# A bidirectional SSD scan split in two parts: exponents and chunk states beside the projections, y beside q, k and v

## The chip, the cores and the metric

The kernel runs on one core of a Trainium2 chip. It is one program for TensorE (PE, with its weight loads as PEld), VectorE (DVE), ScalarE (ACT), GpSimd (POOL) and SyncE (SP), which issues most DMAs; ACT issues the rest. Each engine works through its own instructions in order. The metric is the device time of one execution in microseconds.

## The reference

One block of a hybrid encoder on 1024 tokens of 1024 float32 numbers, depth 1. A combined projection makes z, xBC, dt, q, k and v. An SSD group (16 heads of 64, two groups of 8 heads, state 128, chunks of 128 tokens, both directions) and a neighbourhood attention group work on it, and an output projection and an MLP follow. The part that the change touches:

```
h = rmsnorm(x);  z, xbc, dt_raw, q, k, v = split(h @ w_in)
xs, b, c = split(silu(conv5(xbc)));  dt = softplus(dt_raw + dt_bias)
# ssd_chunked, per direction (the backward one on flipped tokens):
a_cum  = cumsum(dt * a, within a chunk)
decay  = exp(where(lower, a_cum[l] - a_cum[s], -inf))
y_diag = ((c @ b.T) * decay) @ (xs * dt)
state  = b.T @ (xs * dt * exp(a_cum[-1] - a_cum))      # one per chunk
h_in   = scan: h = exp(a_cum[-1]) * h + state
y_off  = (c @ h_in) * exp(a_cum)
y = y_f + y_b + d_skip * xs;  g = rmsnorm(y * silu(z)) per group
x = x + concat(g, neighbourhood_attention(q, k, v)) @ w_out
x = x + relu(rmsnorm(x) @ w1)**2 @ w2
```

## The kernel before

There are 8 chunks c and 2 groups g of 8 heads. Matrices are split into a high and a low part (fp32r), and every product is made by three matmuls (mm3, L179).

The first stage normalises and transposes x. Then `xbc` (L429) makes the twelve column tiles of xBC: 48 matmuls each (px), an eviction to ub, a convolution of four operations on DVE and SiLU on ACT. B and C stay in SBUF (bT, cT, bNh, bNl); xs goes through transposes (ptx) to the DRAM tensor xs_dr. `decays` (L330) runs after the first four tiles: it makes dt and its cumulative sums, keeps the factors c1, e1, ed and wd, and stores the sums to cum_dr (L426). Then z is made in 16 tiles of 24 matmuls (pz, L503 to 512), and its SiLU is stored to sz_dr.

The scan and the projections of q, k and v (pq, L686 to 734, 48 tiles of 24 matmuls) share the next stretch. The scan runs over i = 0 to 7 and both groups: `backward(7 - i, g)` and then `forward(i, g)` (L679 to 682). `backward` makes the part inside a chunk for both directions at once. It takes C B^T (pcb, L589). For each half q of the heads it loads a block of the cumulative sums, broadcast to all partitions (rb from cum_dr, L607, 512 KB, two buffers), subtracts c1 on POOL twice (L614), picks the direction by a mask on DVE (copy_predicated, L620), takes the exponential on ACT (L625), multiplies by C B^T on DVE (L627), and multiplies with xs on TensorE (pd, L632). `carried` (L559) gives a direction's y from its state (py), and `decay_state` (L537) brings the state one chunk further: xw = xs * wd on POOL, a split on ACT and DVE (xh, xl), a product (pS), a decay on POOL (L551), an addition on DVE (L552) and a new split (sh, sl). The two directions meet in the middle, so half of the sums go to DRAM (y1_dr) and come back. `gated` (L572) multiplies with SiLU(z), normalises and stores to y_dr.

The order in which each engine gets its instructions isn't the order of the code: the tile framework schedules the whole program by its own model of durations, and the order is then fixed. TensorE gets pq, pS, py and pd in one mixed row. A tile of a pool is used again when its readers are done; a pool that is opened later may lie on the same memory as one that was closed, and its tiles then wait for the old ones.

Before the scan's loop stand 26 DMAs that build the attention's bias table (t1_dr, t2_dr, L524 to 534), on SP.

Of the kernel before, what the change touches and what calls it, by code (L numbers as in the profile page):

```python
# [56 lines left out]
def hymba_block(  # L57
# [66 lines left out]
    y1_dr = dr.tile([NT, P, D], F32, name="y1_dr")  # L124
# [54 lines left out]
    def mm3(pt, ah, al, bh, bl, first, last):  # L179
        nc.tensor.matmul(pt, lhsT=ah, rhs=bh, start=first, stop=False)  # L180
        nc.tensor.matmul(pt, lhsT=ah, rhs=bl, start=False, stop=False)  # L181
        return nc.tensor.matmul(pt, lhsT=al, rhs=bh, start=False, stop=last)  # L182

# [37 lines left out]
    with ExitStack() as ph:  # L221
# [91 lines left out]
        with ExitStack() as p1:  # L313
            qp = p1.enter_context(tc.tile_pool(name="qp", bufs=2, side="right", reuse_waits="tile"))
# [15 lines left out]
            def decays():  # L330
                wraw = qp.tile([P, KD, 32], F32, tag="smxr", name="wraw", bufs=1)
# [32 lines left out]
                bias = qp.tile([P, 2, 16], F32, name="bias", bufs=1)  # L364
                nega = qp.tile([P, 2, 16], F32, name="nega", bufs=1)
# [6 lines left out]
                def tmp(name):  # L372
                    return qp.tile(sm, F32, tag="sm" + name, name=name, bufs=1)
# [49 lines left out]
                cum = qp.tile([P, 256], F32, name="cum", bufs=1)  # L423
# [71 lines left out]
            decays()  # L495
            for ft in range(8):
                xbc((ft,))


            szb = sz_dr.rearrange("c p f -> (c p) f").rearrange(  # L500
                "(i b j) f -> i b j f", b=8, j=8
            )
# [10 lines left out]

        def hb(v):
            return v.unsqueeze(2).broadcast_to([P, 8, HD])

        def h8(v):
            return v.rearrange("p (e d) -> p e d", d=HD)

        with ExitStack() as p2:  # L520
# [14 lines left out]
            st = [[None, None], [None, None]]  # L535

            def decay_state(d, c, g, xw):  # L537
                prev = st[d][g]
                pS = ps_s("pS")
                xh = qp.tile([P, 512], F32R, tag="xh", name="xh", bufs=1)  # L540
                xl = qp.tile([P, 512], F32R, tag="xl", name="xl", bufs=1)
                nc.scalar.activation(xh, xw, AF.Copy)
                nc.vector.tensor_tensor(xl, xw, xh.bitcast(F32), op=sub)
                mm3(pS, bNh[:, c, g, :], bNl[:, c, g, :], xh, xl, True, True)
                new = prev and prev[0]
                if prev is None:
                    new = qp.tile([P, 512], F32, tag=f"st{d}{g}", name="st", bufs=1)
                    nc.vector.tensor_copy(new, pS)
                else:
                    dec = ed[:, d, c, 8 * g : 8 * g + 8]  # L550
                    nc.gpsimd.tensor_tensor(h8(new), h8(new), hb(dec), op=mul)  # L551
                    nc.vector.tensor_tensor(new, new, pS, op=add)  # L552
                sh = qp.tile([P, 512], F32R, tag=f"sh{g}", name="sh", bufs=1)
                sl = qp.tile([P, 512], F32R, tag=f"sl{g}", name="sl", bufs=1)
                nc.scalar.activation(sh, new, AF.Copy)
                nc.vector.tensor_tensor(sl, new, sh.bitcast(F32), op=sub)
                st[d][g] = (new, sh, sl)

            def carried(d, c, g):  # L559
                py = ps_s("py")  # L560
                ct = cT[:, g, c * P : (c + 1) * P]
                ch = qp.tile([P, P], F32R, tag="ch", name="ch", bufs=2)
                cl = qp.tile([P, P], F32R, tag="cl", name="cl", bufs=2)
                nc.scalar.activation(ch, ct, AF.Copy)
                nc.vector.tensor_tensor(cl, ct, ch.bitcast(F32), op=sub)
                mm3(py, ch, cl, *st[d][g][1:], True, True)
                yo = qp.tile([P, 512], F32, tag="yo", name="yo", bufs=1)
                e = e1[:, d, c, 8 * g : 8 * g + 8]
                nc.vector.tensor_tensor(h8(yo), h8(py), hb(e), op=mul)
                return yo  # L570

# [11 lines left out]
            def backward(c, g):  # L583
                hs = slice(8 * g, 8 * g + 8)
                cs = slice(c * P, (c + 1) * P)
                xs = qp.tile([P, 512], F32, tag="xs", name="xs")
                nc.sync.dma_start(xs, xs_dr[c, :, g * 512 : (g + 1) * 512])
                pcb = ps_s("pcb")
                nc.tensor.matmul(  # L589
                    pcb[:, 0:P], lhsT=bT[:, g, cs], rhs=cT[:, g, cs], start=True, stop=True  # L590
                )
                cb = pcb[:, 0:P]
# [8 lines left out]
                )  # L601
                pd = ps_v("pd")
                for q in range(2):
                    h0 = 8 * g + 4 * q
                    rb = qp.tile([P, 2, 4, P], F32, tag="rb", name="rb", bufs=2)
                    r0 = c * 16 + h0
                    nc.sync.dma_start(  # L607
                        rb.rearrange("p d h s -> p d (h s)"),
                        cum_dr[:, r0 : r0 + 4, :]
                        .rearrange("d h s -> d (h s)")  # L610
                        .partition_broadcast(P),
                    )
                    for d in range(2):
                        nc.gpsimd.tensor_tensor(  # L614
                            rb[:, d],
                            rb[:, d],
                            c1[:, d, c, h0 : h0 + 4].unsqueeze(2).broadcast_to([P, 4, P]),
                            op=sub,
                        )
                    nc.vector.copy_predicated(  # L620
                        rb[:, 0],
                        lmask.unsqueeze(1).broadcast_to([P, 4, P]),
                        rb[:, 1],
                    )
                    nc.scalar.activation(rb[:, 0], rb[:, 0], AF.Exp)  # L625
                    gm = rb[:, 0]
                    nc.vector.tensor_tensor(  # L627
                        gm, rb[:, 0], cb.unsqueeze(1).broadcast_to([P, 4, P]), op=mul
                    )
                    for j in range(4):  # L630
                        e = 4 * q + j
                        nc.tensor.matmul(  # L632
                            pd[:, e * HD : (e + 1) * HD],
                            lhsT=gm[:, j, :],
                            rhs=xs[:, e * HD : (e + 1) * HD],
                            start=True,
                            stop=True,
                        )
                y1 = qp.tile([P, 512], F32, tag="y1", name="y1")
                nc.gpsimd.tensor_tensor(h8(y1), h8(xs), hb(cf), op=mul)  # L640
                if c < NT - 1:
                    yo = carried(1, c, g)
                    nc.gpsimd.tensor_tensor(y1, y1, yo, op=add)
                nc.vector.tensor_tensor(y1, y1, pd, op=add)
                if c >= NT // 2:
# [89 lines left out]

# [680 lines left out]
```

## Time and profile before

| | |
|---|---|
| median of 3 runs | 1672.34 us (1671.72 to 1681.54) |
| the profiled execution | 1682.42 us, of it 1680.6 us in the span |
| mean granted TensorE clock | 0.984 |
| busy in the span | PE 1596.8, PEld 1301.1, DVE 1031.1, ACT 722.1, POOL 727.7 us |
| first and last product of z | 178.6, 267.2 us |
| first and last product of q, k, v | 267.7, 675.9 us |
| DMA | 274.01 MB, 163 GB/s over the span |

A busy time of TensorE holds the latency of its pipeline, so a row of matmuls shows as fully busy even where each comes 0.23 us after the one before and lasts 0.39. In the rows of groups, "out<-in xcount" names what is written and read, then the busy time of the group in us and the mean of one in ns, then the idle time of the engine just before, and what ended it. In the rows of stretches the engines' busy times stand in order, and behind them the granted clock, the busy share of the 16 DMA engines and GB/s. "DMA issues" gives the KB of one transfer and the median time from issue to landing.

### The profile page before, as it was taken

What the parts mean: (1) busy time and instruction counts of PE and PEld (TensorE: products, weight loads), DVE (VectorE), ACT (ScalarE), POOL (GpSimd) and SP (SyncE); (2) the same over time, 40 slices, a digit from 0 to 9 for tenths busy, and PEclk for the clock granted to TensorE, in tenths of its full rate; (3) what the DMA queues carried; (4) which work ended last, traced back from release to release, by engine and by line L of the source; (5) the groups of instructions that cost most, each with busy time, mean ns of one, the idle gap of its engine ahead of it and who ended that gap; (6) DMA issues with size and microseconds to landing.
All of it is one profiled execution on the core that took longest, in us unless ns stands there. A gap on an engine that the chain in (4) does not pass through costs nothing. (4 is left out here: it accounts for less than half of the span.)

```text
span 1680.6 us, 20886 instructions
## 1 busy us (share of the span) xinstructions
PE 1596.8 (95%) x7461; PEld 1301.1 (77%) x7461; DVE 1031.1 (61%) x1438; ACT 722.1 (43%) x1195; POOL 727.7 (43%) x522
## 2 busy tenths in 40 slices
PE   6999999999988889999999989999999979999999
PEld 5788888777776678887887867788888868888887
DVE  5776314788886853566675567444343387887863
ACT  5434223334343432566566533544444544433330
POOL 4000003877787861233335233344444464455551
PEclk9999999999999999999999999999999999999999
DMA  8213336866675885978565241353344386644231
GB/s 207 61 38 104 90 99 195 218 195 186 226 231 176 221 256 192 275 201 221 167 183 169 89 150 51 113 178 136 138 163 151 114 294 243 213 151 150 100 101 75
DMA packets 180290, 274.01 MB, mean 163 GB/s; under 512 B 14603, under 2 KB 105819, under 8 KB 180187
## 3 DMA queue, kind: packets, MB, share of 16 engines
q1 hardware_dynamic: 136203, 231.77, 45.1%
q10 hardware_dynamic: 42976, 37.23, 7.3%
q0 software_dynamic: 1008, 3.67, 0.5%
q8 instruction: 59, 0.97, 0.2%
q14 instruction: 44, 0.36, 0.1%
HBM read 189.40 MB, written 86.56 MB: 164 GB/s over the span
## 5 line engine op out<-in xcount | busy, mean ns | idle before, releaser
L762 POOL TENSOR_TENSOR wl<-wraw,wh 128x1024 fp32r<-128x1024 f32 x110 | 299.7, 2736 | 317.6 <-ACT wh L761 303.1
L761 ACT ACTIVATE wh<-wraw 128x1024 fp32r<-128x1024 f32 x110 | 115.6, 1054 | 151.2 <-PE px L747 51.2
L747 PE MATMUL px<-wh,ahl 128*128 128x512 f32 x512 | 160.8, 391 | 4.6 <-ACT ahl L761 3.3
L180 PE MATMUL pq<-wh,hTh 128*128 128x512 f32 x384 | 154.3, 404 | 5.7 <-ACT wh L150 5.6
L181 PE MATMUL pq<-wl,hTh 128*128 128x512 f32 x384 | 153.8, 402 | 3.8 <-DVE wl L151 3.8
L747 PE MATMUL px<-h,wh 128*128 128x512 f32 x496 | 156.0, 396 | 1.4 <-DVE x L1103 1.4
L182 PE MATMUL pq<-wh,hTl 128*128 128x512 f32 x384 | 153.4, 401 | 0.0
L762 DVE TENSOR_TENSOR ahl<-ar,ahl 128x1024 fp32r<-128x1024 f32 x56 | 115.1, 2062 | 22.9 <-ACT ahl L761 21.8
L761 ACT ACTIVATE ahl<-ar 128x1024 fp32r<-128x1024 f32 x56 | 58.2, 1052 | 140.0 <-PE px L747 74.7
L747 PEld LDWEIGHTS px<-wh,ahl 128*128 128x128 f32 x512 | 96.0, 188 | 25.9 <-ACT ahl L761 3.7
L747 PEld LDWEIGHTS px<-h,wh 128*128 128x128 f32 x496 | 93.2, 188 | 24.0 <-ACT h L186 1.6
L151 DVE TENSOR_TENSOR wl<-wraw,wh 128x1024 fp32r<-128x1024 f32 x40 | 54.0, 1355 | 82.3 <-ACT wh L150 81.7
L747 PE MATMUL px<-wl,ahl 128*128 128x512 f32 x256 | 99.8, 390 | 0.0
L747 PE MATMUL px<-h,wl 128*128 128x512 f32 x248 | 98.1, 396 | 0.0
L180 PEld LDWEIGHTS pq<-wh,hTh 128*128 128x128 f32 x384 | 74.1, 193 | 22.2 <-ACT wh L150 7.2
L181 PEld LDWEIGHTS pq<-wl,hTh 128*128 128x128 f32 x384 | 74.0, 193 | 20.9 <-DVE wl L151 6.2
L614 POOL TENSOR_TENSOR rb<-rb,c 128x512 f32<-128x512 f32 x64 | 76.6, 1218 | 21.8 <-DMA rb<-cum_dr 21.7
L182 PEld LDWEIGHTS pq<-wh,hTl 128*128 128x128 f32 x384 | 73.9, 192 | 15.2
L186 ACT ACTIVATE pth<-ptp 128x384 fp32r<-128x384 f32 (+1 forms) x128 | 56.8, 456 | 67.3 <-PE ptp L961 66.7
L747 PE MATMUL pz<-h,wh 128*128 128x512 f32 x256 | 82.0, 401 | 0.7 <-DVE h L187 0.7
L150 ACT ACTIVATE wh<-wraw 128x1024 fp32r<-128x1024 f32 x58 | 61.1, 1056 | 46.3 <-PE px L181 19.2
L747 PE MATMUL pz<-wh,ahl 128*128 128x512 f32 x256 | 80.5, 390 | 0.0
(271 smaller groups left out, 4087.5 us busy)
## 6 DMA issues: line engine op xcount, KB each, us to landing
ar<-act_dr SPq DMA_DIRECT2D x56, 512.0 KB, 3.7
act_dr<-cq SPq DMA_DIRECT2D x49, 512.0 KB, 3.2
wraw<-in_w_in_dram SPq DMA_DIRECT2D x44, 512.0 KB, 4.5
rb<-cum_dr SPq DMA_DIRECT2D x32, 512.0 KB, 7.1
wraw<-in_w_mlp_in_dram SPq DMA_DIRECT2D x32, 512.0 KB, 4.6
wraw<-in_w_mlp_out_dram SPq DMA_DIRECT2D x32, 512.0 KB, 5.5
q_dr<-hl ACTq DMA_DIRECT2D x64, 128.0 KB, 3.2
k_dr<-hl ACTq DMA_DIRECT2D x16, 512.0 KB, 5.3
```

The costliest lines, as they stand in the source:

```text
L150: nc.scalar.activation(hi[:, 0:n], raw[:, 0:n], AF.Copy)
L151: lo_eng.tensor_tensor(lo[:, 0:n], raw[:, 0:n], hi[:, 0:n].bitcast(F32), op=sub)
L180: nc.tensor.matmul(pt, lhsT=ah, rhs=bh, start=first, stop=False)
L181: nc.tensor.matmul(pt, lhsT=ah, rhs=bl, start=False, stop=False)
L182: return nc.tensor.matmul(pt, lhsT=al, rhs=bh, start=False, stop=last)
L186: nc.scalar.activation(hi, src, AF.Copy)
L614: nc.gpsimd.tensor_tensor(rb[:, d], rb[:, d], c1[:, d, c, h0 : h0 + 4].unsqueeze(2).broadcast_to([P, 4, P]), op=sub,)
L747: nc.tensor.matmul(pt, lhsT=a, rhs=b, start=f, stop=l, skip_group_check=True)
L761: nc.scalar.activation(hl[0], src, AF.Copy)
L762: eng.tensor_tensor(hl[1], src, hl[0].bitcast(F32), op=sub)
```

## The change

The scan is split. The exponents that `backward` made, up to the mask but without the exponential, are made by `segment` and stored to a DRAM tensor seg_dr: four blocks after each of the eight x tiles in the code. The chunk states of both directions are made by `state`, one chunk of each direction after each of the first 14 tiles of z, and every state that a chunk starts from is stored to st_dr. Each pS is told to stand behind the z tile's last product (`issue_after`).

The rest is one step per chunk and group, first all of g = 0, then all of g = 1. `prepare` loads xs, the two exponent blocks and the states, takes the exponential on ACT and splits C and the states. `inside` makes C B^T, both directions' py, the product of exponents and C B^T, and sums y in SBUF. `finish` makes pd behind a tile of q, k or v, and gates. `prepare` of the next step is called ahead of `finish`, and two or three tiles of q, k and v are made per step. y1_dr, with its 14 stores and 14 loads, is gone. The small tiles of `decays` now lie inside two tiles (`room`) that have the exponents' tag rb, so that both use the same two buffers.

By count the program keeps its matmuls. C is split 16 times in place of 28. SP has 120 DMAs more: 32 stores and 32 loads of exponents, 28 and 28 of states, 14 more loads of xs, and 14 loads of y1 less; ACT issues 14 stores less.

```diff
+            def segment(g, c, q):
+                h0 = 8 * g + 4 * q
+                rb = rp.tile([P, 2, 4, P], F32, tag="rb", name="rb")
+                r0 = c * 16 + h0
+                nc.sync.dma_start(
+                    rb.rearrange("p d h s -> p d (h s)"),
+                    cum_dr[:, r0 : r0 + 4, :]
+                    .rearrange("d h s -> d (h s)")
+                    .partition_broadcast(P),
+                )
+                for d in range(2):
+                    nc.gpsimd.tensor_tensor(
+                        rb[:, d],
+                        rb[:, d],
+                        c1[:, d, c, h0 : h0 + 4].unsqueeze(2).broadcast_to([P, 4, P]),
+                        op=sub,
+                    )
+                nc.vector.copy_predicated(
+                    rb[:, 0],
+                    lmask.unsqueeze(1).broadcast_to([P, 4, P]),
+                    rb[:, 1],
+                )
+                nc.sync.dma_start(
+                    seg_dr[g, c, :, q], rb[:, 0].rearrange("p h s -> p (h s)")
+                )
+
+            segs = [(g, c, q) for g in range(2) for c in range(NT) for q in range(2)]
             for ft in range(8):
                 xbc((ft,))
+                for sg in segs[4 * ft : 4 * ft + 4]:
+                    segment(*sg)
...
+            def state(d, c, g, xs, mark):
+                hs = slice(8 * g, 8 * g + 8)
+                xw = qp.tile([P, 512], F32, tag="xw", name="xw")
+                nc.gpsimd.tensor_tensor(h8(xw), h8(xs), hb(wd[:, d, c, hs]), op=mul)
+                xh = qp.tile([P, 512], F32R, tag="xh", name="xh")
+                xl = qp.tile([P, 512], F32R, tag="xl", name="xl")
+                nc.scalar.activation(xh, xw, AF.Copy)
+                nc.vector.tensor_tensor(xl, xw, xh.bitcast(F32), op=sub)
+                pS = ps_s("pS")
+                with tc.issue_after(mark):
+                    mm3(pS, bNh[:, c, g, :], bNl[:, c, g, :], xh, xl, True, True)
+                prev = st.get((d, g))
+                new = qp.tile([P, 512], F32, tag=f"st{d}", name="st")
...
+                st[d, g] = new
+                nc.sync.dma_start(st_dr[d, g, c + 1 - 2 * d], new)
...
                     for k in range(KD):
                         s = (slice(None), k, slice(t * P, (t + 1) * P))
-                        mm3(pt, hTh[s], hTl[s], *get(k), k == 0, k == KD - 1)
+                        mark = mm3(pt, hTh[s], hTl[s], *get(k), k == 0, k == KD - 1)
...
+                    if 8 * g + t < 14:
+                        states(8 * g + t, mark.ins)
...
+                for q in range(2):
+                    gm = qp.tile([P, 4, P], F32, tag=f"gm{q}", name="gm")
+                    nc.sync.dma_start(gm.rearrange("p h s -> p (h s)"), seg_dr[g, c, :, q])
+                    nc.scalar.activation(gm, gm, AF.Exp)
+                    gms.append(gm)
...
+            for n, (c, g) in enumerate(steps):
+                xs, gms, chl, sts = held
+                y1 = inside(c, g, *held)
+                if n + 1 < len(steps):
+                    held = prepare(*steps[n + 1])
+                mark = next(units)
+                finish(c, g, xs, gms, y1, mark)
+                for _ in range(1 + n % 2):
+                    mark = next(units)
```

The order on SP, from the store of the cumulative sums on. xs_dr takes the x tiles, wraw are weights of z. Before:

```order
L426 DMA cum_dr_75<-cum_711 128x128 x2
L149 DMA wraw_1383<-in_w_in_dram 128x2x512
L488 DMA xs_dr_70<-xn_783 128x8x128
L488 DMA xs_dr_70<-xn_865 128x8x128
L149 DMA wraw_1389<-in_w_in_dram 128x2x512
L488 DMA xs_dr_70<-xn_947 128x8x128
```

And now, where each rb tile is a block of exponents (two buffers, taken in turn):

```order
L446 DMA cum_dr_76<-room_611 128x128 x2
L521 DMA rb_794<-cum_dr_76 128x2x512
L521 DMA rb_800<-cum_dr_76 128x2x512
L150 DMA wraw_1576<-in_w_in_dram 128x2x512
L508 DMA xs_dr_70<-xn_780 128x8x128
L539 DMA seg_dr_71<-rb_794 128x512
L521 DMA rb_806<-cum_dr_76 128x2x512
L539 DMA seg_dr_71<-rb_800 128x512
L508 DMA xs_dr_70<-xn_886 128x8x128
L521 DMA rb_812<-cum_dr_76 128x2x512
```

A block's load stands behind the store of the block that had its buffer, and the x tiles' stores stand between them.

On TensorE, at the same place in z, behind its 115th product. Before, z goes on alone, from one weight tile (wh, wl) to the next:

```order
L181 MATMUL pz_1507<-wl_1385,hTh_90 128x512
L182 MATMUL pz_1507<-wh_1384,hTl_91 128x512
L180 MATMUL pz_1507<-wh_1390,hTh_90 128x512
L181 MATMUL pz_1507<-wl_1391,hTh_90 128x512
L182 MATMUL pz_1507<-wh_1390,hTl_91 128x512
```

Now the first two chunk states stand there, one for each direction:

```order
L181 MATMUL pz_1826<-wh_1583,hTh_91 128x512
L181 MATMUL pS_1624<-xh_1620,bNh_98 128x512
L182 MATMUL pz_1826<-wl_1584,hTh_91 128x512
L181 MATMUL pS_1639<-xh_1635,bNh_98 128x512
L182 MATMUL pS_1624<-xl_1621,bNh_98 128x512
L183 MATMUL pS_1624<-xh_1620,bNl_99 128x512
```

Of the 84 products of pS, 69 stand in z and 15 among the first 63 products of q.

On POOL, behind the x tiles' small fills. Before, nothing stood there until the scan:

```order
L435 MEMSET ub_1295 128x2
L436 MEMSET ub_1295 128x2
L523 MEMSET zt_1871 128x192
L640 TENSOR_TENSOR y1_1930<-xs_1899,cf_1905 128x512
L655 TENSOR_TENSOR xw_1934<-xs_1899,wd_103 128x512
```

Now, within z, exponent blocks (rb), weighted inputs (xw) and decayed states (st) take turns:

```order
L528 TENSOR_TENSOR rb_1230<-rb_1230,c1_101 128x512 x2
L567 TENSOR_TENSOR st_1762<-st_1702,ed_103 128x512
L554 TENSOR_TENSOR xw_1812<-xs_1810,wd_104 128x512
L567 TENSOR_TENSOR st_1806<-st_1746,ed_103 128x512
L554 TENSOR_TENSOR xw_1856<-xs_1854,wd_104 128x512
L528 TENSOR_TENSOR rb_1236<-rb_1236,c1_101 128x512 x2
```

Fifteen blocks stand on POOL and DVE ahead of the first xw and xl, and twelve more before the xw of the last state that z's part of TensorE's order needs.

More of the change, by code (lines that the diff above doesn't have):

```diff
@@ L330, in decays, with slot @@
             def decays():
-                wraw = qp.tile([P, KD, 32], F32, tag="smxr", name="wraw", bufs=1)
+                room = [rp.tile([P, 4, 256], F32, tag="rb", name="room") for _ in range(2)]
+                slots = ["xr", "na", "u", "tt", "t2", "pl", "la", "cum"]
+                def slot(name):
+                    i = slots.index(name)
+                    return room[i // 4][:, i % 4]
+                wraw = slot("la").rearrange("p (k f) -> p k f", f=32)
                 nc.sync.dma_start(
@@ L500, in hymba_block, with states @@
+            def states(n, mark):
+                g, i = n // 7, n % 7
+                for d, c in ((0, i), (1, NT - 1 - i)):
+                    xs = qp.tile([P, 512], F32, tag="xs", name="xs")
+                    nc.sync.dma_start(xs, xs_dr[c, :, g * 512 : (g + 1) * 512])
+                    state(d, c, g, xs, mark)
+            pa.close()
+            qp = p1.enter_context(tc.tile_pool(name="zv", bufs=2, side="right", reuse_waits="tile"))
             szb = sz_dr.rearrange("c p f -> (c p) f").rearrange(
@@ L534, in hymba_block @@
                 )
[L535 to L570, printed above, removed]
             def gated(y1, c, g):
@@ L601, in backward @@
                 )
-                pd = ps_v("pd")
[L603 to L631, printed above, removed]
@@ new lines, in inside @@
+                y1 = qp.tile([P, 512], F32, tag="y1", name="y1")
+                nc.gpsimd.tensor_tensor(h8(y1), h8(xs), hb(cf), op=mul)
+                for gm in gms:
+                    nc.vector.tensor_tensor(
+                        gm, gm, cb.unsqueeze(1).broadcast_to([P, 4, P]), op=mul
+                    )
+                for d in sts:
+                    yo = qp.tile([P, 512], F32, tag="yo", name="yo")
+                    nc.vector.tensor_tensor(h8(yo), h8(pys[d]), hb(e1[:, d, c, hs]), op=mul)
+                    nc.gpsimd.tensor_tensor(y1, y1, yo, op=add)
@@ L632, in backward, with finish @@
+                return y1
+            def finish(c, g, xs, gms, y1, mark):
+                pd = ps_v("pd")
+                with tc.issue_after(mark):
+                    for e in range(8):
                         nc.tensor.matmul(
                             pd[:, e * HD : (e + 1) * HD],
-                            lhsT=gm[:, j, :],
+                            lhsT=gms[e // 4][:, e % 4, :],
                             rhs=xs[:, e * HD : (e + 1) * HD],
@@ new lines, in hymba_block @@
+            units = qkv_units()
+            steps = [(c, g) for g in range(2) for c in range(NT)]
+            held = prepare(*steps[0])
+            mark = next(units)
[7 more added lines that the diff above has]
+                for _ in range(1 + n % 2):
+                    mark = next(units)
@@ L743, in hymba_block @@
+            for mark in units:
+                pass
     ORD = (1, 2, 6, 5, 7, 3, 4)
```

161 lines of the change are left out of this document (80 added, 81 removed).

## The prediction

> **What bounds the kernel now.** I read the slices of the page first, then the stretches around the scan, then who waits for whom on TensorE.
>
> ```profile
> span 1680.6 us, 20886 instructions
> PE   6999999999988889999999989999999979999999
> ```
>
> ```profile
> core 0: us, PE busy (x) PEld busy (x) DVE busy (x) ACT busy (x) POOL busy (x), PEclk, DMA share, GB/s
> 130.00:267.50 137.50, 137.50 (x640) 114.46 (x639) 49.62 (x44) 45.19 (x55) 0.70 (x9) 1.00 0.34 95
> 267.50:676.00 408.50, 372.68 (x1748) 300.10 (x1747) 289.68 (x419) 155.48 (x271) 285.63 (x266) 0.97 0.73 215
> ```
>
> TensorE is the bound nearly everywhere. The weak place is 267.5 to 676, in which the scan runs beside q, k and v: 35.8 us idle (408.5 - 372.7), and a granted clock of 0.97, which costs 12 us of 408.5. Just before it, in 130 to 267.5 (last x projections and z), TensorE never stops, DVE is busy for 36% and POOL for 0.7 us. The change carries work from the second stretch into the first.
>
> How long must the second stretch be? Rows of the timeline give the rate, and three groups the small products:
>
> ```profile
> 270.16 0.39 PE L181 MATMUL pq<-wl,hTh 128*128 128x512 f32 x1
> ...
> 272.65 0.39 PE L180 MATMUL pq<-wh,hTh 128*128 128x512 f32 x1
> ```
>
> ```profile
> L632 PE MATMUL pd<-xs,rb 128*128 128x64 f32 x256 | 33.2, 278 | 7.7 <-DVE rb L627 6.8 <-issue 0.6
> L476 PE MATMUL ptx<-ident,acc 128*128 128x128 f32 x64 | 8.4, 272 | 0.0
> ```
>
> From 270.16 to 272.65 are 11 intervals: a 128x512 product takes 0.226 us of TensorE, whatever its 0.39 us of latency. The stretch has 1152 of pq, 84 of pS and 84 of py: 1320 x 0.2264 = 299 us. With 33 for pd and 17 for the 128 transposes of q and k (32 groups of four, at 8.4/16 each) it needs about 350 of its 408. So 58 us are loss, and this is all that the change can win there. The waits say whose loss:
>
> ```profile
> PE pcb L589 <- DVE yo L569: 7.7, 4, 2.9
> PE pd L632 <- DVE rb L627: 6.8, 6, 2.3
> PE pq L180 <- ACT wh L150: 5.6, 3, 2.9
> PE pq L181 <- DVE wl L151: 3.8, 6, 1.2
> PE pcb L589 <- DVE st L552: 3.0, 1, 3.0
> PE py L180 <- DVE st L552: 1.6, 2, 1.4
> PE ptq L707 <- DVE qn L701: 1.5, 3, 0.9
> PE pS L180 <- ACT rb L625: 1.4, 2, 0.8
> PE py L181 <- DVE sl L556: 0.9, 2, 0.6
> PE pS L180 <- DVE st L552: 0.9, 1, 0.9
> ```
>
> The scan's own waits (pcb, pd, py, pS) are 7.7 + 6.8 + 3.0 + 1.6 + 1.4 + 0.9 + 0.9 = 22.3 of the 35.8 us. The weights' (wh, wl) are 9.4; these stay.
>
> **Part by part: the scan behind its preparation.** The carried recurrence leaves this stretch, and 69 of the 84 pS products (15.6 us of TensorE) go to z, which is neutral. Of the 58 us I let the scan's share go, 22.3/35.8 = 62%: 36 us. Bounds: 22 (only the named waits), and 48 (all but the weights' 9.4). What can come late instead is pd: its exponents are now loaded, go through ScalarE's exponential and DVE's product with cb, and ScalarE and DVE have q, k and v's evictions queued behind a late load. The first step also follows the last stored exponents, and sixteen bias copies on the same queue stand ahead of its second half:
>
> ```profile
> 276.08 12.52 SPq L531 DMA_DIRECT2D t_dr<-t_dr  x16
> ```
>
> I take 3 us for it all, from nothing (loads are asked for one step ahead, some 21 us) up to 2 us in each of 16 steps, 32. The net gain of the stretch is 33 us, between -10 and 48.
>
> **The exponents beside the projections.** Now what hangs on segment. One exponent block is a load of 512 KB, two subtractions on POOL, one copy_predicated on DVE, and a store of 256 KB, and with two rb buffers its buffer is loaded again only when that store has landed. Before, no store stood in this loop. The rows:
>
> ```profile
> 128.70 0.81 SPq L426 DMA_DIRECT2D cum_dr<-cum  x2
> 399.67 1.26 SPq L607 DMA_DIRECT2D rb<-cum_dr  x2
> 420.11 0.41 SPq L607 DMA_DIRECT2D rb<-cum_dr  x1
> ```
>
> ```profile
> 405.54 2.04 POOL L614 TENSOR_TENSOR rb<-rb,c 128x512 f32<-128x512 f32 x2 [3.61 <-DMA rb<-cum_dr]
> 426.18 2.04 POOL L614 TENSOR_TENSOR rb<-rb,c 128x512 f32<-128x512 f32 x2 [0.92 <-DMA rb<-cum_dr]
> ```
>
> ```profile
> L614 POOL TENSOR_TENSOR rb<-rb,c 128x512 f32<-128x512 f32 x64 | 76.6, 1218 | 21.8 <-DMA rb<-cum_dr 21.7
> L620 DVE COPY_PREDICATED rb<-lmask,rb 128x512 f32<-128x512 int32 x32 | 41.7, 1304 | 16.2 <-POOL rb L614 16.2
> L620 DVE COPY_PREDICATED rb<-lmask,rb x32: 714/1554/1827, 280.4 to 598.6; 128x512 f32<-128x512 int32 x32
> L551 POOL TENSOR_TENSOR st<-st,ed 128x512 f32<-128x512 f32 x24 | 28.3, 1180 | 0.6 <-DVE sl L556 0.6
> L655 POOL TENSOR_TENSOR xw<-xs,wd 128x512 f32<-128x512 f32 x14 | 15.1, 1079 | 2.8 <-DMA xs<-xs_dr 2.8
> L542 ACT ACTIVATE xh<-xw 128x512 fp32r<-128x512 f32 x28 | 17.5, 625 | 39.5 <-PE pS L182 12.0 <-POOL xw L655 8.1 <-PE pq L182 5.2
> ```
>
> ```profile
> rb<-cum_dr SPq DMA_DIRECT2D x32, 512.0 KB, 7.1
> wraw<-in_w_in_dram SPq DMA_DIRECT2D x44, 512.0 KB, 4.5
> sz_dr<-zs ACTq DMA_DIRECT2D x16, 256.0 KB, 2.8
> y_dr<-y ACTq DMA_DIRECT2D x24, 256.0 KB, 5.4
> ```
>
> POOL, idle and waiting for the load, began 5.9 and 6.1 us after the issue: 6.0. Two subtractions take 2.0, the copy 1.3, a store of this size 2.8 (sz_dr, written in the quiet z stage), two issues 0.8. The loop is 12.9 us, so 6.5 us per block. Bounds: 4.5 + 2.0 + 0.7 + 2.8 + 0.8 = 10.8, and 7.1 + 2.4 + 1.3 + 5.4 + 0.8 = 17.0.
>
> The order puts fifteen blocks on POOL and DVE ahead of the first chunk state, and TensorE's first pS behind 115 of z's products. cum_dr is issued by 129.5 and should land about 132 (2.8 us, as sz_dr). The fifteenth block is the eighth turn of its buffer: 132 + 7 x 12.9 + 6.0 + 2.0 + 1.3 = 231.6. Then xw (1.1) and xh (0.6): pS can start at 233. z begins at 178.6:
>
> ```profile
> L180 PE MATMUL pz<-wh,hTh x128: 389/389/481, 178.6 to 267.0; 128*128 128x512 f32 x128
> ```
>
> Without waits TensorE is at its first pS at 178.6 + 115 x 0.2264 + 2.1 (16 transposes) = 207. It stalls 26 us (bounds: 10 with the short loop, 57 with the long). The same lateness reaches it by DVE too, whose convolutions and evictions are queued behind the copies; I count it once.
>
> From there to the end of z: TensorE has 269 pz + 69 pS = 338 x 0.2264 = 76.5 us. POOL has 24 subtractions, 23 xw and 18 decays: 24 x 1.22 + 23 x 1.08 + 18 x 1.18 = 75 us. The block loop has 12 turns of 6.5, 77 us. All three are level, so nothing hides anything. The transfers are worse: 12 x 0.79 MB of blocks, 23 xs and some 22 states of 0.26, 11 sz of 0.26 and about 2 MB of weights make 26 MB. The scan's stretch moved 215 GB/s at a share of 0.73, which is 294 at one: 88 us. I add 12 us here, from 0 up to 12 x 8.5 - 76.5 = 25.
>
> ```profile
> 620.00:640.00 20.00, 16.31 (x70) 12.85 (x69) 9.10 (x11) 6.25 (x9) 7.67 (x7) 0.91 1.10 336
> ```
>
> (This row is the most that the trace moved, 336 GB/s; at that rate the 26 MB take 77 us.) So z ends 38 us later than its work asks, between 10 and 82.
>
> The Trainium skill, "DMA: Bandwidth & Descriptors", section "Anatomy of one DMA — SWDGE (gpsimd) path", puts a transfer at about 2.0 us plus its bytes at 436 GB/s; an estimate from that page is 3.2 us for the load and 2.6 for the store, a loop of 9.9 and a stall of 3 us in place of 26, and the sum would then be 3 + 12 - 33, a gain of 18 us. The trace disagrees for this load: 5.9 and 6.1 us.
>
> Other edits: 14 saves and 14 loads of y1 go, 12 splits of C go, 120 DMAs come on SP; the sizes stand in the terms above. The NA stage and the MLP keep their order and cost.
>
> **The sum.** +26 + 12 - 33 = +5 us against the profiled execution: 1682.4 + 5 = 1687. Its span is 1680.6 with 1.8 around it, and the median of the runs shown, 1672.3, lies 10 below it; on that scale the forecast is 1677. A measurement of this kernel can tell about 1% (17 us) from no change.
>
> **Rivals.** *The blocks are short enough* (the side of a gain): with the loop of 10.8 the stall is 10 us, and at 336 GB/s the rest of z costs 1; with the 36 us of the scan's own waits gone and no new one, 10 + 1 - 36 = -25: 1647. For: the new loads come one at a time rather than in pairs, and the share around 130 to 267.5 was 0.34; the page named above says the same. Against: both quoted loads stand in the stretch with a share of 0.73, and this change brings the x and z stage to the same or above. It decides below a loop of about 11.5 us. *The block loop is long*: stores land like y_dr (5.4) and loads like the group's 7.1, 17.0 in all: 57 + 25 - 33 = +49, 1721. It becomes slower by more than 1% from a loop of about 14 us, 1.1 more than I take. For: 26 MB in 77 to 88 us is the fullest DMA of the program. *The scan finds a new wait*: pd waits 2 us in each step, or the first y step starts late: 38 - 36 + 32 = +34, 1706. For: ScalarE now waits in its queue for a load in each step; against: 21 us of notice. That the work is not moved is excluded by the order.
>
> **Chances and range.** Forecast 0.38 (its own range 1656 to 1689, within 1%), short blocks 0.30, long blocks 0.21, new wait in the scan 0.11. Hence faster 0.30, same 0.38, slower 0.32. The range cuts the ends of both sides: 1640 to 1712.
>
> **What would show it.** In the profile after: POOL idle in the x and z stage for "DMA rb<-cum_dr", spaced 6.5 us; the first pS near 233 and the last z product near 320 where work alone gives 283; a stretch of q, k, v and y of about 355 us with the waits of pcb, pd and py for st, sl and rb gone, and those for wh and wl left. A first pS near 215 means short blocks, one past 250 long ones. I am wrong in kind if z stays unbroken, or if the scan's stretch still loses over 50 us.

## The result, and the profile after

The changed kernel takes 1703.74 us (median of 4 runs, 1699.28 to 1705.71) against 1672.77 us before (4 runs on the same chip): a ratio of 1.0163, with an interval of 1.0140 to 1.0186. It is slower by 1.6%, inside the range, but not the case that I held the likeliest. The profiled execution took 1705.05 us, 1703.3 of them in the span, 22.6 more than the profiled one before.

The first two parts of the page after, the span and TensorE's slices:

```profile
span 1703.3 us, 21105 instructions
PE   6999778998999998999999989899999979999999
```

The shallow hole of the kernel before (the 8s of slices 12 to 15, in the scan) is gone; a deeper one stands in slices 5 to 7, ahead of and in z. Four stretches show where the time went. The columns are those of the prediction's rows; first the kernel before, then the changed one:

```profile
130.00:200.00 70.00, 70.00 (x341) 58.55 (x340) 42.27 (x38) 29.57 (x36) 0.70 (x9) 1.00 0.39 110
200.00:240.00 40.00, 40.00 (x179) 33.15 (x178) 4.90 (x4) 9.06 (x11) 0.00 (x0) 1.00 0.35 99
240.00:430.00 190.00, 178.24 (x844) 144.19 (x843) 130.43 (x193) 66.79 (x110) 123.78 (x111) 0.97 0.69 194
430.00:700.00 270.00, 245.29 (x1149) 197.48 (x1147) 175.75 (x264) 108.08 (x200) 170.65 (x162) 0.97 0.73 218
```

```profile
130.00:200.00 70.00, 61.92 (x289) 50.42 (x288) 47.52 (x44) 25.60 (x30) 25.69 (x28) 0.98 0.68 188
200.00:240.00 40.00, 23.67 (x92) 18.59 (x91) 11.58 (x12) 5.92 (x9) 12.64 (x12) 0.77 0.71 181
240.00:430.00 190.00, 166.65 (x701) 129.19 (x701) 125.72 (x154) 61.22 (x97) 135.23 (x116) 0.93 0.89 275
430.00:700.00 270.00, 264.30 (x1323) 222.38 (x1322) 149.31 (x244) 106.06 (x179) 113.59 (x119) 0.99 0.69 209
```

From 430 us on TensorE hardly stops any more: 264 of 270 us busy, against 245. Before 430 it loses far more. The tiles of the changed kernel say where (min, median and longest ns, first and last start):

```profile
L181 PE MATMUL pz<-wh,hTh x128: 388/390/777, 188.7 to 332.6; 128*128 128x512 f32 x128
...
L181 PE MATMUL pS<-xh,bNh x28: 386/394/795, 236.4 to 359.3; 128*128 128x512 f32 x28
...
L183 PE MATMUL pq<-wh,hTl x384: 387/390/629, 337.3 to 697.3; 128*128 128x512 f32 x192
```

z begins 10 us later than before (178.6), the first pS comes at 236.4, and z ends at 333. TensorE's waits, first from 120 to 320 us (x and z), then from 320 to 720 (the scan):

```profile
PE pS L181 <- ACT xh L557: 14.1, 4, 10.1
PE ptx L496 <- ACT acc L488: 12.3, 3, 6.0
```

```profile
PE pq L181 <- DVE hl L195: 5.7, 1, 5.7
PE py L181 <- DMA q_dr<-hl: 4.6, 1, 4.6
PE pq L182 <- DVE wl L152: 3.7, 4, 2.0
PE pS L181 <- ACT xh L557: 2.0, 2, 1.6
PE pd L689 <- DVE gm L676: 1.4, 1, 1.4
```

ptx waits for the convolution, pS for the chain xw, xh behind the exponent blocks. The convolution is late because VectorE stands idle in front of masked copies whose block POOL has not finished (21.6 us from 130 to 210), with the convolution's operations (acc) next in its queue. VectorE's rows, and TensorE's behind them:

```profile
DVE rb L534 <- POOL rb L528: 21.6, 7, 6.3
```

```profile
199.41 0.76 DVE L534 COPY_PREDICATED rb<-lmask,rb 128x512 f32<-128x512 int32 x1 [3.78 <-POOL rb L528]
200.05 2.61 DVE L484 SCALAR_TENSOR_TENSOR acc<-ub,pcol,acc 128x1024 f32<-128x1024 f32 x2
206.46 0.73 DVE L534 COPY_PREDICATED rb<-lmask,rb 128x512 f32<-128x512 int32 x1 [3.80 <-POOL rb L528]
207.07 2.59 DVE L484 SCALAR_TENSOR_TENSOR acc<-ub,pcol,acc 128x1024 f32<-128x1024 f32 x2
```

```profile
210.81 1.97 PE L496 MATMUL ptx<-ident,acc 128*128 128x128 f32 x8 [5.99 <-ACT acc L488]
```

The scan's chains of pcb, pd and py are gone but for single waits.

**One measure for all runs.** Every kernel here gives TensorE the same products. I give each instruction of the trace the usual distance to the next of its kind (0.226 us for a 128x512 product; 1523 us in all, the same for all kernels), add these up for what has started by a time t, and take the sum from t. What is left I call the fall-behind. It counts waits and slow clock alike, in the profiled execution:

```
us behind at t =        130   200   240   430   700   first pS  copies after 240
before                   24    24    24    48    90     280.8
after                    25    36    56    98   109     236.4      17
```

The last column counts the exponent blocks whose masked copy comes after 240 us. So of the 85 us that the changed kernel loses from 130 to 700 us, 11 lie by 200 us, 20 from there to 240 (waits of 6.0 us for ptx and 10.3 for the first pS, and slow products behind both), 42 between there and 430, and 12 in the rest; before it was 0, 0, 24 and 42. That is 19 us more; the other 4 of the 23 come outside this stretch. These are single executions: that of the kernel before lies 9.7 us above its median, so a difference to its row is uncertain by as much, that of half_load_four below lies 7 us under its median and that of one_subtraction 6 above.

### The profile page after: what moved, and what is told of

The parts are those of the page before. It is cut to its first block, busy times and chain, and to the rows that moved or that the text cites. A ratio compares the mean times of both kernels' runs of the same rounds, so it can differ in the third digit from the quotient of the medians.

```text
span 1703.3 us, 21105 instructions
## 1 busy us (share of the span) xinstructions
PE 1599.2 (94%) x7461; PEld 1304.5 (77%) x7461; DVE 1027.5 (60%) x1426; ACT 718.5 (42%) x1183; POOL 724.1 (43%) x522
## 5 line engine op out<-in xcount | busy, mean ns | idle before, releaser
L534 DVE COPY_PREDICATED rb<-lmask,rb 128x512 f32<-128x512 int32 x32 | 38.9, 1216 | 81.3 <-POOL rb L528 78.1
L906 POOL TENSOR_TENSOR mb<-braw,nam 128x256 f32<-128x256 f32 (+1 forms) x48 | 38.5, 832 | 114.4 <-DVE nmx L963 57.1
L151 ACT ACTIVATE wh<-wraw 128x1024 fp32r<-128x1024 f32 x58 | 60.6, 1054 | 55.6 <-DMA wraw<-in_w_in_dram 21.6
```

Source lines behind the costliest of these rows:

```text
L151: nc.scalar.activation(hi[:, 0:n], raw[:, 0:n], AF.Copy)
L534: nc.vector.copy_predicated(rb[:, 0], lmask.unsqueeze(1).broadcast_to([P, 4, P]), rb[:, 1],)
L906: nc.gpsimd.tensor_tensor(mb[:, s].rearrange("p (s r c) -> p s r c", r=16, c=8), v[:, a:b], nam[:, s].rearrange("p (s r c) -> p s r c", r= ...
```

## The experiments

Each run stands beside runs of the kernel before on its chip; the ratio is to these, with its interval. All start from the changed kernel; the last three of the list make the exponents in the scan.

```
                        us      ratio (interval)          130   200   240   430   700   first pS  copies after 240
the change            1703.7   1.0163 (1.0140-1.0186)      25    36    56    98   109     236.4      17
three_buffers         1682.0   1.0027 (1.0012-1.0043)      26    41    57    78    93     241.9      13
four_buffers          1684.3   1.0042 (1.0025-1.0058)      23    41    57    77    91     235.8       8
one_subtraction       1686.8   1.0063 (1.0041-1.0084)      24    40    59    83    98     234.3      14
late_blocks_two       1706.3   1.0182 (1.0146-1.0217)      24    36    40    95   114     215.8      19
late_blocks_four      1682.3   1.0035 (1.0021-1.0048)      23    41    48    77    91     225.9      14
late_blocks_four_8    1683.5   1.0043 (1.0028-1.0058)      24    35    39    78    91     214.6      20
half_load_four        1672.7   0.9968 (0.9951-0.9985)      23    41    58    64    77     237.9       3
no_store_four         1676.5   0.9992 (0.9976-1.0008)      22    44    58    70    84     247.5       2
half_load_late        1676.3   0.9995 (0.9979-1.0011)      24    30    34    72    87     209.5      19
transfers_only        1696.1   1.0124 (1.0103-1.0144)      23    23    43    65   100     223.3
states_only           1668.1   0.9947 (0.9930-0.9965)      22    22    23    44    76     202.0
states_two_ahead      1665.8   0.9933 (0.9911-0.9955)      22    23    23    44    70     202.1
```

**More buffers, less work on POOL, and the exponents back in the scan.** four_buffers and three_buffers give the exponents' tag more buffers:

```diff
-                rb = rp.tile([P, 2, 4, P], F32, tag="rb", name="rb")
+                rb = rp.tile([P, 2, 4, P], F32, tag="rb", name="rb", bufs=4)
```

> Exponent blocks turn on four buffers in place of two; nothing else is edited. Theory LOOP (each buffer's round of load, POOL, VectorE, store and next load, 13.4 us measured in the changed kernel, holds the z stage): four buffers give 13.4/4 = 3.4 us a block; the order now has 23 blocks ahead of the first state's xw on POOL, so the first pS comes about 131 + 23 x 3.4 + 5 = 214 us (236 in the changed kernel) and the other nine blocks fit beside z, whose last product comes near 290 (333); time about 1665 us (1655 to 1680). Rival POOL (its own 75 us of subtractions and 28 xw in the z stage hold it) and rival BYTES (about 26 MB between 200 and 335 us at some 300 GB/s hold it): the work and the bytes are the same, so the first pS may be earlier but z's last product stays past 320, and the time stays at 1690 to 1705.

> Exponent blocks turn on three buffers. LOOP: 13.4/3 = 4.5 us a block, 20 blocks ahead of the first xw in the order, first pS near 131 + 20 x 4.5 + 5 = 226 us, the other 12 blocks take 54 us beside 77 us of z; last product of z near 305, time about 1678 us, between two buffers and four. POOL and BYTES: 1690 to 1705, as with four.

one_subtraction makes half of POOL's subtractions:

```diff
-                for d in range(2):
+                for d in range(1):
                     nc.gpsimd.tensor_tensor(
```

> Each exponent block makes one subtraction on POOL in place of two (the backward direction's is left out, so the exponents above the diagonal are not the reference's); buffers, loads and stores as in the changed kernel. LOOP: a buffer's round is 1 us shorter (12.4), 6.2 us a block; the order has 17 blocks ahead of the first xw, where the changed kernel has 15, so the first pS comes near 131 + 17 x 6.2 + 5 = 241 us, no sooner than now (236); time 1695 to 1708 us. POOL: 32 x 1.2 = 38 us of its work gone, about 20 of it in the z stage: last product of z near 312, time 1675 to 1685. BYTES: unchanged, 1700 to 1706.

states_only takes `segment` and seg_dr out; `prepare` loads and makes the exponents itself:

```diff
-                    gm = qp.tile([P, 4, P], F32, tag=f"gm{q}", name="gm")
-                    nc.sync.dma_start(gm.rearrange("p h s -> p (h s)"), seg_dr[g, c, :, q])
+                    rb = qp.tile([P, 2, 4, P], F32, tag=f"gm{q}", name="rb")
...
+                    gm = rb[:, 0]
+                    nc.vector.copy_predicated(
...
                     nc.scalar.activation(gm, gm, AF.Exp)
```

> The chunk states stay beside z and the scan keeps its one pass, but the exponents are made in the scan again, one step ahead, from the cumulative sums, with their two subtractions, the masked copy and the exponential; nothing is stored of them. LOOP: z is unbroken but for a few us (first pS near 210 us, last product of z 275 to 285). If the scan's gain of 30 us comes from the new order of the pass (ORDER), the scan stretch stays at 360 to 368 us and the time is 1645 to 1658. If it comes from the exponents' having left the scan (EXPONENTS), the scan stretch goes back to 390 to 408 us and the time is 1672 to 1690.

Two buffers more take 1.2 points off, so the round of a buffer was part of the cost; but four buffers end 4 us above LOOP's range and 6 below that of POOL and BYTES, and LOOP named the wrong place. It had counted the planner's new order (23 and 20 blocks ahead of the first xw in place of 15) and still expected the first pS at 214 and 226. It stays at 236 and 242, for a block took some 4.4 us with four buffers and 5.4 with three, not 3.4 and 4.5. one_subtraction speaks against LOOP, which expected no gain: 1.0 point, or 17 us, of the 19 to 29 us that POOL promised. From 240 to 430 us that kernel falls behind by 25 us in place of 42. It makes 14 blocks there, so 14 subtractions of some 1.0 us less on POOL.

states_only shows the price of the exponents' new place: with them in the scan the kernel is 0.5% faster than before. Its z is unbroken:

```profile
L180 PE MATMUL pS<-xh,bNh x28: 390/393/393, 202.0 to 290.8; 128*128 128x512 f32 x28
...
L180 PE MATMUL pq<-wh,hTh x384: 387/389/792, 284.7 to 661.2; 128*128 128x512 f32 x192
```

The scan stretch, 376.5 us, lies between the two theories' bounds: 32 us less than before (where 78 pS, 18 us, have moved to z), and still 15 more than with the change. Of TensorE's loss from 240 to 700 us, 65 before, the states' leaving and the new order of the pass take 12 (to 53), if the 9.7 us by which that execution was long lie elsewhere. The exponents' leaving takes up to 34 more (half_load_four below, with nearly all blocks made by 240, loses 19 there), but they have to be made somewhere.

**Another order.** If the blocks ahead of the first xw set its time, fewer of them there should help. These three tie later blocks on POOL behind the xw of a z tile:

```diff
-                for sg in segs[4 * ft : 4 * ft + 4]:
+                for sg in segs[16 * ft // 8 : 16 * (ft + 1) // 8]:
                     segment(*sg)
...
+                    with tc.issue_after(held[0]):
+                        for sg in late[n * 1 // 1 : (n + 1) * 1 // 1]:
+                            segment(*sg)
```

> Four exponent buffers, and the order changed: 16 blocks are made beside x's projections, the other 16 are tied on POOL one behind each z tile's second xw, so 16 blocks stand ahead of the first xw there and not 23. All else as in the changed kernel. Theory ORDER (the first pS comes when the blocks that POOL's order puts ahead of the first xw are through: 15 x 6.7 us with two buffers, 20 x 5.4 with three, 23 x 4.4 with four, so near 235 us every time): 131 + 16 x 4.4 + 5 = 207 us for the first pS, one block per z tile of 6.0 us needs 4.4, so z runs unbroken, last product of z near 300 us, scan stretch 350 to 355, time 1652 to 1665 us. Rival BYTES (the loads and stores, not the order, hold z): same bytes, last product of z past 318, time 1680 to 1690 as with four buffers alone. Rival DVE (the masked copies crowd VectorE beside x's convolution, and z's start moves from 179 to 189 us for it): z still starts at 189 to 193 here.

> As the one before, but only 8 blocks beside x's projections, and three behind every two z tiles. ORDER: first pS 200 to 207 us; 24 blocks in 107 us of z and states leave 4.5 us each, just what four buffers gave (4.4), so last product of z 288 to 305, time 1650 to 1668. DVE: z's start comes back to 179 to 184 us, since half the masked copies are left beside the convolution. BYTES: the bytes move into z (24 blocks, 18.9 MB there, 63 us at 300 GB/s, beside some 20 MB of its own): last product of z past 325, time 1690 or more.

> The changed kernel's two buffers, only the order changed: 10 blocks beside x's projections, one tied behind each z tile's second xw, the last six behind z. ORDER: first pS 131 + 10 x 6.7 + 5 = 203 to 210 us (236 now), then 6.7 us a block against 6.0 us a tile with its two states, so z's last product near 305 us (333); the six blocks behind it end about 345, beside the scan's first steps, which need only the first blocks; time 1665 to 1685 us (1704). BYTES: no better than 1695.

ORDER got its early part and lost the rest. With 8 blocks ahead the first pS comes at 214.6, and TensorE is 39 us behind at 240 in place of 57. By 430 it is 78 behind, as with four buffers in the planner's order (77), and the time is the same. late_blocks_two, too, gains 16 us by 240 and has lost 13 of them by 430. So what the blocks cost doesn't go away when they are moved; it is paid where they are made. DVE's bet on z's start wasn't put to the test: with 8 blocks ahead z still began at 189.5, but the changed kernel, with its two buffers, gets no more than 8 masked copies done before its z begins at 188.7 (four_buffers 12, with z at 192.5).

**Bytes or work.** Two kernels take 8.4 MB away, by half a load or by no store:

```diff
-                    rb.rearrange("p d h s -> p d (h s)"),
-                    cum_dr[:, r0 : r0 + 4, :]
+                    rb[:, 0:1].rearrange("p d h s -> p d (h s)"),
+                    cum_dr[0:1, r0 : r0 + 4, :]
```

> Four exponent buffers; each block loads 256 KB in place of 512 KB: the forward sums alone, from which both directions' exponents are made by the same two subtractions (so the backward exponents are not the reference's, and the exponential scales them down to stay finite). Instructions, copies and stores otherwise as with four buffers. So far TensorE, with the time of its products taken away, falls behind by 54 us between 130 and 430 us with four buffers in three different orders, and by 73 and 70 with two buffers in two orders. Theory BYTES (the transfers between 130 and 430 us, 72 to 77 MB at a DMA share up to 1.0, hold TensorE): 8.4 MB less at 270 GB/s is 31 us less, a fall-behind of 23 to 35 us, time 1655 to 1668 us. Theory ROUND (what counts is how long a block takes from load to reload, 18 us with four buffers): only the load's landing gets shorter, by 1 to 2 us of 18, so 5 us at most; time 1677 to 1685. Theory VECTORE/POOL (their work): no change, 1680 to 1686.

> Four exponent buffers; the exponents' store is left out, and the scan loads x's rows in place of them (same size, so the outputs of the scan are not the reference's). BYTES: again 8.4 MB less, so as the half load: fall-behind 23 to 35 us, time 1655 to 1668. ROUND: the store and the next load's wait for it (5 to 11 us of 18) go, so a block comes every 2.7 us at most and the first pS may come at 215 us, and the gain is larger than the half load's: 1650 to 1665. VECTORE/POOL: no change.

The half load comes nearest to BYTES (1.0042 to 0.9968), though short of its range (41 us of fall-behind between 130 and 430), and no_store_four gains less than either theory gave it. But the planner had changed its order again: 29 blocks stand ahead of the first xw with the half load, all 32 without the store. Both kernels lose as much by 240 us as four_buffers, and less than 3 us from 260 to 430, where no block is left. The bytes had to be taken away in an order that keeps blocks in z:

> The half load (256 KB a block, backward exponents not the reference's) put into the order with 8 blocks beside x and three behind every two z tiles. The half load with the planner's own order lost 39 us of its 41 by 260 us, ahead of the 29 blocks that stood before its first xw, and 3 after that; the late order with full loads lost 11 by 200 us and 43 from there to 430. Theory BYTES: with fewer bytes the late order's loss from 200 us on shrinks to 5 to 20 us, and its early gain is kept: fall-behind between 130 and 430 us 15 to 31 us, time 1648 to 1664. Theory WORK (the subtractions, copies and states on POOL and VectorE, which are the same in number here, set the pace of z and the first scan steps): 43 us again, fall-behind 50 to 54, time 1678 to 1685.

From 200 to 430 us it falls behind by 42.6 us, where nearly the same order with full loads lost 42.8: WORK's number, and BYTES is out for this stretch with four buffers; with two a half load wasn't run. (The time, 1676.3, is 2 us under WORK's range and 12 above that of BYTES. The half point that it gains over late_blocks_four_8 lies elsewhere, 5 us of it beside x.) What fills it shows in POOL's groups of half_load_late between 240 and 330 us (busy us, mean ns | idle before them):

```profile
L528 POOL TENSOR_TENSOR rb<-rb,c 128x512 f32<-128x512 f32 x30 | 40.2, 1350 | 0.1
L556 POOL TENSOR_TENSOR xw<-xs,wd 128x512 f32<-128x512 f32 x19 | 26.2, 1391 | 0.9 <-DMA xs<-xs_dr 0.9
L571 POOL TENSOR_TENSOR st<-st,ed 128x512 f32<-128x512 f32 x18 | 25.2, 1405 | 0.0
```

The subtractions, xw and the states' decay keep POOL busy for 89 of 90 us. A z tile with two states and one and a half blocks asks POOL for 4 x 1.40 + 3 x 1.35 = 9.7 us, and TensorE for 6.8 (24 products and 6 of pS at 0.226); POOL sets the pace. TensorE feels it in its waits for xh and xl, and for the weights' wl, since VectorE stands 18.0 us in front of masked copies for POOL. With the changed kernel's two buffers the same groups read:

```profile
L528 POOL TENSOR_TENSOR rb<-rb,c 128x512 f32<-128x512 f32 x24 | 27.5, 1164 | 18.2 <-DMA rb<-cum_dr 10.2 <-issue 5.4 <-DMA xs<-xs_dr 2.6
L554 POOL TENSOR_TENSOR xw<-xs,wd 128x512 f32<-128x512 f32 x20 | 26.2, 1320 | 1.2 <-DVE xl L558 0.6 <-DMA xs<-xs_dr 0.5
L567 POOL TENSOR_TENSOR st<-st,ed 128x512 f32<-128x512 f32 x17 | 21.8, 1285 | 0.0
```

Its work is 75.5 us, and it stands idle for 18.2 us in front of subtractions, 10.2 of them by the profile for a block's load, with the next xw queued behind. Both add up. The table's last column goes the same way: from 240 to 430 us TensorE loses some 2 us for each block left with three or four buffers (39/20, 39/19, 29/14, 20/8, 21/13, 6/3), 1.8 with one subtraction and two buffers (25/14), and 2.5 to 2.9 with both subtractions on two (42/17, 55/19). This is no clean price of a block: waits of the scan lie in it too. Counted only to just behind each kernel's last masked copy it is 0.9 to 1.6 with more buffers, and 1.7 and 2.1 with two and both subtractions; four_buffers, whose last copy starts at 283, loses 12 of its 20 us after 340. no_store_four doesn't fit (12 us with 2 blocks), for its first pS only comes at 247.5.

**The transfers by themselves.** To states_only I added the changed kernel's loads and stores, with nothing done on them:

```diff
+                nc.sync.dma_start(
+                    rb.rearrange("p d h s -> p d (h s)"),
+                    cum_dr[:, r0 : r0 + 4, :]
...
+                nc.sync.dma_start(
+                    seg_dr[g, c, :, q], rb[:, 0].rearrange("p h s -> p (h s)")
+                )
```

> The kernel with the states beside z and the exponents in the scan, to which the changed kernel's transfers are added and nothing else: beside x and z 32 loads of 512 KB and 32 stores of 256 KB turn on four buffers, with no subtraction and no copy on them, and nobody reads what they store (so the result is the reference's). Without them TensorE falls behind by 1 us between 130 and 300 us, and the time was 1668 us. BYTES: 25.2 MB more by about 300 us, where the loads of weights and x have to share: TensorE falls behind by 20 to 45 us there; time 1688 to 1712. WORK: the transfers alone cost TensorE nothing, under 5 us; time 1665 to 1673.

BYTES named the time (1696.1) and the size of the loss, but for the most part it isn't the sharing that it had in mind. Beside x the transfers cost nothing, though the share was 0.94 there; TensorE then loses 20 us by 240, 18.3 of them in one wait, and 2 or 3 more up to 340. (The scan, too, loses more than in states_only, 54 us from 340 to 700 against 43; why is open.) The stretches, and that wait:

```profile
130.00:190.00 60.00, 60.00 (x293) 50.20 (x292) 41.29 (x37) 24.95 (x30) 0.51 (x8) 1.00 0.94 280
190.00:250.00 60.00, 40.72 (x174) 32.53 (x173) 10.92 (x14) 11.19 (x18) 14.93 (x13) 0.86 0.96 310
250.00:340.00 90.00, 90.00 (x401) 73.69 (x400) 55.05 (x67) 30.33 (x46) 59.10 (x51) 1.00 0.76 247
```

```profile
PE pS L181 <- ACT xh L545: 18.3, 1, 18.3
```

What came late are the loads of xs for the first states, queued on SP behind the blocks' loads and stores (for whose turns SP waits 29.9 and 10.6 us between 130 and 230). In states_only the first is issued at 192.5, here at 212.1, and its xw starts 5.8 and 9.4 us after that: the queue makes some 20 us of the delay, the slower landing 4 (rows of the xs loads, first of states_only, then of transfers_only):

```profile
L548 SPq DMA_DIRECT2D xs<-xs_dr x28: 319/320/1031, 192.5 to 274.7; - x28
```

```profile
L566 SPq DMA_DIRECT2D xs<-xs_dr x4: 319/375/1121, 212.1 to 223.6; - x4
```

So the 11 us that the changed kernel loses beside x don't come from a busy DMA as such. They come with the blocks that are made there: by z's start it has lost 10 us with 8 masked copies, one_subtraction 12 with 9, four_buffers 16 with 12, half_load_four 17 with 15; only half_load_late, with half the load, gets away with 6 for 8. In the changed kernel the rows above show how: VectorE waits in its queue for a block, and the convolution behind it. How much of this is waiting and how much the copies' own time wasn't parted. The 10 us in front of its first pS may come by either queue, and its trace can't part them: SP issues the first xs at 225.4 (8.0 us to land), and POOL has block 15 behind it at 234.7, level with that x.

```profile
225.37 1.04 SPq L578 DMA_DIRECT2D xs<-xs_dr  x2
...
232.66 2.04 POOL L528 TENSOR_TENSOR rb<-rb,c 128x512 f32<-128x512 f32 x2 [6.23 <-DMA rb<-cum_dr]
234.65 2.50 POOL L554 TENSOR_TENSOR xw<-xs,wd 128x512 f32<-128x512 f32 x2
```

A version with the xs loads on another queue would part them; it wasn't tried.

**A version that beats both.** states_two_ahead is states_only with three buffers for each half's exponents and their preparation two steps ahead:

> The states beside z and the exponents in the scan, but made two steps ahead in place of one (three buffers for each half). With one step ahead TensorE fell behind by 52 us between 300 and 700 us, ptq waiting 12.5 us for VectorE's qn, py 4.3 and hl 4.0 among it. If the exponents' latency holds the scan: the fall-behind drops to 25 to 40 us and the time to 1640 to 1656. If VectorE's and POOL's queues hold it (the exponents' operations stand ahead of qn, hl there): no change, 1662 to 1672.

It is faster than before by 0.7%, and its interval overlaps that of states_only: the exponents' lead is at most a small part of what holds the scan (from 240 to 700 us it loses 47 us, against 53).

## Why the prediction was right and wrong

**The first pS, +26.** The mechanism was right and the size near. One buffer's turn, from the trace of the changed kernel: its first block's load is issued at 131.49, its eighth (block 15) at 224.96, so 93.5/7 = 13.4 us against 12.9.

```profile
131.49 0.88 SPq L521 DMA_DIRECT2D rb<-cum_dr  x2
...
224.96 0.36 SPq L521 DMA_DIRECT2D rb<-cum_dr  x1
```

```profile
seg_dr<-rb SPq DMA_DIRECT2D x32, 256.0 KB, 4.2
```

The store, which I priced at 2.8 from a quiet stage, took 4.2; the copy beside x took 0.75 in place of 1.3. The first pS came at 236.4 (233). The loss by then is 31 us in place of 26. Only 10 of it are the wait for the first pS; 12 are waits of ptx, by the second path that the prediction names, VectorE's queue. "I count it once" was right as a sum. What it didn't see is that a shorter loop need not bring the first pS forward: with three and four buffers the planner put 20 and 23 blocks in front of it in place of 15.

**The rest of z, +12.** This is the step that failed, by its size and by its reason. I found POOL (75 us), the block loop (77) and TensorE (76.5) level and took the transfers, at 88 us, as what sets the pace. From 240 us to the first product of q at 335 TensorE falls behind by 20 us in place of 12, and half_load_late shows, with four buffers, that bytes are not what counts there. In the changed kernel POOL's 75.5 us of work and its 18.2 of waits stand in one queue and add up, so the ring of POOL, loop and TensorE did not overlap to its longest part; that this sum makes just the 20 us is argued from these rows, not shown by a run on two buffers. The scan's first steps went on paying: 22 us more up to 430.

**The scan, -33.** By the same measure the stretch from z's end to q, k and v's end lost 63 us before and 33 now, the 22 just named among them: 30 gained. The waits of pcb for st and yo are gone, pd waits 1.4 us once, wl's 3.7 stayed, and the stretch is 362 us long where I named 355.

**The sum.** 31 + 20 - 30 = +21 against my +5, with 22.6 measured between the profiled executions. The rest of the miss, 8 us, is the scale: the execution profiled before lay 9.7 us above its median, the one after only 1.3 above, and I had taken 10 off as if both would.

**The rivals.** *Short blocks* needed a loop below 11.5 us and fell. The Trainium skill's page "DMA: Bandwidth & Descriptors", section "Anatomy of one DMA — SWDGE (gpsimd) path", gave a loop of 9.9; 13.4 was measured. *Long blocks* named the right sign, by a loop of 17 that didn't come. *A new wait in the scan* of 2 us in each step didn't come either; what is new there are single waits (hl 5.7, q_dr 4.6). The time ended between the forecast and the long blocks, 15 us above the forecast's own range (to 1689).

## What to carry to other kernels

Work that is moved into a quiet stretch is paid for on the engine that makes it, so count that engine's queue with its waits in it: an in-order engine that must wait for one transfer holds up all that stands behind, as VectorE held the convolution here. When loop, engine and transfers come out level, add up what shares one queue rather than take the longest. And where a planner sets the order, a faster part may be answered by another order, so compare kernels by what is left at fixed points of time, not by one wait.

## What the runs showed of the hardware

**VectorE's masked copy takes twice as long while POOL works.** Copies of the changed kernel beside x (130 to 190 us) and in z (250 to 330 us), the same 128x512 form:

```profile
L534 DVE COPY_PREDICATED rb<-lmask,rb x8: 724/755/1650, 139.4 to 184.9; 128x512 f32<-128x512 int32 x8
...
L534 DVE COPY_PREDICATED rb<-lmask,rb x10: 1550/1574/1627, 248.5 to 323.4; 128x512 f32<-128x512 int32 x10
```

In z, where POOL goes on to its next operation at once, all ten take 1.55 us or more; beside x, where it mostly waits for the next block, the median is 0.76. Two of the ten, with POOL's operations around them:

```profile
264.57 1.04 POOL L567 TENSOR_TENSOR st<-st,ed 128x512 f32<-128x512 f32 x1
264.64 1.57 DVE L534 COPY_PREDICATED rb<-lmask,rb 128x512 f32<-128x512 int32 x1 [1.97 <-POOL rb L528]
265.57 1.50 POOL L554 TENSOR_TENSOR xw<-xs,wd 128x512 f32<-128x512 f32 x1
...
307.68 1.04 POOL L554 TENSOR_TENSOR xw<-xs,wd 128x512 f32<-128x512 f32 x1
307.71 1.63 DVE L534 COPY_PREDICATED rb<-lmask,rb 128x512 f32<-128x512 int32 x1 [1.93 <-POOL rb L528]
```

The copy starts while an operation of POOL runs, and ends 0.60 and 0.62 us after that one ends; POOL's operation takes its usual 1.04 us, and the next one, which starts under the copy, 1.50. So the two take turns by whole operations, and the copies are alike because POOL's subtraction, which releases each, also lets POOL's next one start. The Trainium skill's page "SBUF — State Buffer", section "SBUF: two separate sides", says that the two engines share a pair of ports, which the first takes for a whole instruction while the other stands still. The trace agrees: the copy's 1.57 us are 0.97 up to the end of POOL's operation and 0.60 of its own. POOL's subtraction takes 1.02 us by itself and 1.35 in half_load_late's full stretch.

**A wait of TensorE costs clock behind it.** The granted clock was 0.77 from 200 to 240 us, where TensorE waited 6.0 and 10.1 us in one piece each (0.52 from 210 to 215, right behind the first), and single products of z took up to 777 ns there against 481 at most before. The Trainium skill's page "TensorE: Matmul & The Clock Gate", section "What's actually happening", has the array at half rate after an idle window of about 3.4 us; the doubled products agree.

**Transfers at a share of 0.94 did not touch TensorE.** 280 GB/s beside x cost it nothing in transfers_only, as long as no load that TensorE needed stood behind them in SP's queue.
